# The first stage of a hybrid encoder layer: who loads the vectors, how the early weight columns arrive, and in what order x is turned

## The chip, the cores and the metric

One core of a Trainium2 chip runs the whole program. The metric is device time in microseconds (us); the kernel before took 2727.44 us (median of three runs, 2724.23 to 2729.16). TensorE (PE) multiplies, with weight loads shown apart (PEld); VectorE (DVE), ScalarE (ACT) and GpSimd (POOL) work beside it; SyncE (SP) issues most DMAs. Everything is float32, and each large product is made of float32r pieces.

## The reference

One layer for 512 prompt frames and 64 sample frames (two independent sequences, with their own condition vectors c), model width 2048:

```python
mod = silu(c) @ w_ada + b_ada                 # (2, 6*2048): sh1, sc1, g1, sh2, sc2, g2
h   = rmsnorm(x, norm1) * (1 + sc1) + sh1
proj = h @ w_in                               # columns a_q, a_k, a_v, a_r, a_lr, b_q, b_k, ...
# gated linear attention and gated DeltaNet on the columns of proj, heads normed and gated
x = x + g1 * (concat(o_a, o_b) @ w_out)
h = rmsnorm(x, norm2) * (1 + sc2) + sh2
x = x + g2 * conv_ffn(h)                      # w_up, causal conv of width 3, silu, w_down
y = rmsnorm(x, final_norm)                    # plus the new recurrent and conv states
```

The change touches only the first stage: `mod` (its parts sh1 and sc1), `h`, and the first columns of `proj`.

## The kernel before, in words

**Layout.** h is held transposed: 16 tiles k of 128 model columns by 576 frames (two halves of 288). A product of one weight tile 128x128 with one h tile is six matmuls (`mm6`, L735): weight and h are each split into a rounded high part and a remainder (`wh`, `wl`; `hh`, `hl`), and wh·hh, wh·hl, wl·hh are summed, for two halves each. ACT makes the high part, DVE the remainder (`pair_split`, L1132; `shift_x`, L767).

**The first stage** is `head` (L857). It does three things that depend on one another:

- *x*: five row blocks (four of 128 prompt frames, one of 64 sample frames) are loaded in four pieces each (`x_load`, L866). ACT squares them for the row sums (`x_square`), GpSimd takes the power -1/2 of each block's mean (`x_norm`, through `rsqrt`, L188), PE turns the blocks into xT (`x_turn`, L897), and the results in PSUM are copied out by ACT and DVE in turn. `x_lengths` (L889) spreads the row factors over all partitions into `rb`, which needs all five powers.
- *modulation* (`modulation`, L960): the columns of w_ada for sc1 and sh1 pass through PE in 48 pieces ("ada pieces": `hraw<-in_w_ada` loads and `bank<-hraw,cs` matmuls). After the four pieces of one half, DVE copies the sums (`rw`, L984), PE transposes them (`bank<-consts,rw`, L2423), DVE reduces and adds b_ada (`msum`, `mod`), and for sc1 makes `s`. Then DVE makes `tmp` = xT·s·rb (`scale_x`, L762), and ACT and DVE make `hh` and `hl`.
- *early products*: six column blocks of 128 columns (EARLY, L57) and 66 narrow columns (`ps_nar`, L1262) are multiplied with h while h comes into being. The 16 h tiles go in six groups of 2, 2, 3, 4, 3, 2 (GROUPS, L56), called group 0 to 5 here. For each group three pairs of column blocks are loaded (`pair_load`, L1122), split and multiplied, and the ada pieces of the next group are spread between these products (`product`, L1066).

**What sets the order.** Each engine runs its own queue in order. The order on each comes from the order of the code, moved by a scheduler that places an instruction by its estimate of when its inputs are there; a few are tied by hand (`issue_after`). SP's queue is in order, too, and a load waits there until its buffer is free: 9 buffers `hraw` (w_ada pieces and narrow weights, in a ring), 3 buffers `raw` for pairs. Seven groups of small vectors (c, b_ada, norms, conv weights, states) are loaded by `v_load` as rows (L811) and turned into columns by `v_turn` (PE L819, DVE L820).

**GpSimd before** has little to do here: memsets, then the reload of its code that precedes the powers (the second ISA row below), then the five powers.

Of the kernel before, what the change touches and what calls it, by code (L numbers as in the profile page):

```python
# [16 lines left out]
P = 128  # L17
# [39 lines left out]
EARLY = (("q", OFF_BQ, 0), ("aq", OFF_AQ, 0), ("ak", OFF_AK, 0), ("aq", OFF_AQ, 1), ("ak", OFF_AK, 1), ("aq", OFF_AQ, 2))  # L57
# [57 lines left out]
class Kern:  # L115
# [673 lines left out]
    def load_vectors(self):  # L789
# [17 lines left out]
        def load(g):  # L807
            rt = self.hslot(places[g], [P, P])
            at = 0
            for name, ap, n in groups[g]:  # L810
                nc.sync.dma_start(rt[at:at + n], ap)  # L811
                self.vmap[name] = cols[:, g, at:at + n]
                at += n
            rows_of[g] = rt, at
# [13 lines left out]
    def raw(self):  # L828
        return self.wp.tile([P, 1024], F32, tag="raw", bufs=3, name=self.name("raw"))

# [26 lines left out]
    def head(self, pool):  # L857
# [5 lines left out]
        xt, ms, squared = {}, {}, []  # L863
# [9 lines left out]
        def x_square(b):  # L873
            n = P if b < 4 else TS
            ms[b] = pool.tile([P, 8], F32, tag="ms4", bufs=5, name=self.name("ms4"))
            for q in range(4):
                A.activation(junk[:n], xt[b][q][:n], AF.Square, scale=float(D) ** -0.5, accum_out=ms[b][:n, q:q + 1])
                squared.append(last())
# [18 lines left out]
        def x_turn(b):  # L897
            n = P if b < 4 else TS
            per = 4 if b < 4 else 8
            for k0 in range(0, KD, per):  # L900
                ps = self.pgt()[:, 0]
                for k in range(k0, k0 + per):
                    with self.tc.issue_after(summed[0]) if summed else nullcontext():
                        T.transpose(ps[:, (k - k0) * n:(k - k0 + 1) * n], xt[b][k // 4][:n, k % 4 * P:(k % 4 + 1) * P],
                                    self.c["ident"][:n, :n])
                even = k0 // per % 2 == 0
                put = (lambda o, x: A.activation(o, x, AF.Copy)) if even else V.tensor_copy
                ahead = 4 * b + (8 if k0 // per < 2 else 10)
                with self.tc.issue_after(squared[min(len(squared), ahead) - 1]):
                    if b < 4:  # L910
                        put(xT[:, k0:k0 + per, b // 2, (b % 2) * P:(b % 2 + 1) * P], ps.rearrange("p (k t) -> p k t", k=per))
                    else:
                        for h in range(2):
                            put(xT[:, k0:k0 + per, h, HP:HT], ps.rearrange("p (k h t) -> p k h t", k=per, h=2)[:, :, h])
# [10 lines left out]
        v_turn(0)  # L925

# [23 lines left out]
        def ada_fill():  # L950
            while len(got) < len(todo):
                if len(got) % 8 == 0:
                    g = len(got) // 8
                    w_ahead(3 if g == 1 else 3 * g - 2)
# [5 lines left out]
        def modulation(g):  # L960
# [3 lines left out]
            for n0 in range(8 * g, 8 * g + 8, together):  # L964
# [13 lines left out]
                summed[:] = [last]  # L978
# [39 lines left out]
        first, summed, self.split_of = modulation(0), [], None  # L1018
        ada_ahead(2)
        x_load(3)  # L1020
        x_load(4)
        ada_ahead(4)
        v_load(1)
        ada_ahead(7)
        w_ahead(1)
        nar = self.narrow_load(*GROUPS[0])
        x_square(0)
        x_norm(0)
        x_square(1)
        for b in range(5):  # L1030
            if b < 4:
                x_norm(b + 1)
# [3 lines left out]
            x_diag(b)  # L1036
            if b > 0:
                next(first)
            if b == 3:
                v_turn(1)  # L1040
        x_lengths()
        for k in range(2):
            scale(k)
# [11 lines left out]
        w_ahead(2)  # L1055
        ps_nar = self.ps_nar = self.pm.tile([P, 2, 512], F32, tag="nar", bufs=1, name="ps_nar")
        accs = [pool.tile([P, 2, HT], F32, tag=f"acc{e}", bufs=1, name=f"acc{e}") for e in range(len(EARLY))]

        for g, (m0, nm) in enumerate(GROUPS):
            ks = range(m0, m0 + nm)  # L1060
            end = g == len(GROUPS) - 1
            mods = iter(()) if end else modulation(g + 1)
            units = nm * len(EARLY)
            done = stepped = 0

            def product(e, j, k):  # L1066
                nonlocal done, stepped
# [3 lines left out]
                while stepped < 7 and (stepped - 1) * (units - nm - 2) < 6 * done:  # L1071
                    r = next(mods, None)
                    stepped += 1
                    if stepped == 4 and not end:
                        for i in range(2):
                            scale(m0 + nm + i)
                    if r is WAIT:
                        break

            for e in range(0, len(EARLY), 2):  # L1080
                w = begun.pop(0) if begun else self.pair_split(*raws[3 * g + e // 2])
                ps = [self.pgt() for _ in range(2)]
                if e == 0:
                    for k in ks:
                        if k == len(self.h):
                            make(k)
                        self.mm_narrow(k, nar[:, k - m0])
                        for j in range(2):
                            product(e, j, k)
                        if k == ks[1]:  # L1090
                            w_ahead(3 * g + 3)
# [7 lines left out]
                for j in range(2):  # L1099
                    if e == 4 and not end and j == 0:  # L1100
                        nar = self.narrow_split(pool, self.narrow_load(*GROUPS[g + 1]))
                        begun.append(self.pair_split(*raws[3 * g + 3]))
                        self.split_of = last()
                    for k in ks:
# [7 lines left out]
                        if k == ks[1] and j == 0:  # L1112
                            w_ahead(3 * g + e // 2 + 3)
# [8 lines left out]
    def pair_load(self, offs, k0, n):  # L1122

        raw, w = self.raw(), n * P
        for e, off in enumerate(offs):
            self.nc.sync.dma_start(raw[:, e * w:(e + 1) * w].rearrange("p (k n) -> p k n", k=n), self.w_in(off)(k0, k0 + n))
# [5 lines left out]
    def pair_split(self, raw, n, order=None):  # L1132
# [9 lines left out]
        return [[x[:, e * w:(e + 1) * w].rearrange("p (k n) -> p k n", k=n) for x in (hi, lo)] for e in range(2)]  # L1142
# [1380 lines left out]
```

## Time and profile before

| | |
|---|---|
| median of three runs | 2727.44 us |
| profiled execution, own time | 2728.48 us |
| its span | 2726.8 us |
| PE busy | 2676.9 us (98%) |
| DVE busy | 2292.5 us (84%) |
| ACT busy | 1295.6 us (48%) |
| POOL busy | 479.1 us (18%) |
| DMA moved | 487.84 MB, 179 GB/s in the mean |
| first 175 us: DMA moved | 53.80 MB, 307 GB/s |

The rest of the page says where in these numbers to look: PE is busy in nearly every slice of the span but the first, and DMA is 90% busy in the first two of 40 slices only. The views used below are the windows (busy time of each engine, granted TensorE clock, DMA share and GB/s for one stretch), the timeline (start, length, instruction, and in brackets the idle time of that engine before it and what ended it), the groups by line, and the DMA issues. Times within the kernel count from the span's start.

### The profile page before, as it was taken

Reading aid. Unit: us, or ns where it says so; the run is one execution under the profiler, and the core shown is the slowest. Engines: PE = TensorE matmul, PEld = TensorE weight load, DVE = VectorE, ACT = ScalarE, POOL = GpSimd, SP = SyncE. Lnnn points to the kernel's source line nnn. Section 1 sums busy time; section 2 is a strip of 40 time slices with the busy share of each in tenths; the row PEclk is TensorE's granted clock in tenths of the full one; section 3 lists DMA queues with packets and bytes.
Section 4 is the critical chain, followed back from the end, with each engine's and each line's share of the span. In section 5 each row is a group of like instructions: output and inputs, shape, how many; then the busy total and the mean of one; then the engine's idle time right before and its main releaser. Section 6 shows DMA issues by size and latency. Waiting matters only on the chain.

```text
span 2726.8 us, 52222 instructions
## 1 busy us (share of the span) xinstructions
PE 2676.9 (98%) x20208; PEld 2612.6 (96%) x20208; DVE 2292.5 (84%) x3744; ACT 1295.6 (48%) x2316; POOL 479.1 (18%) x459
## 2 busy tenths in 40 slices
PE   7999999999999999999999999999999999999998
PEld 5699999999999999999999999999999999999998
DVE  4579899988898895688999999999999976888996
ACT  4246454555554442554545454545454544333453
POOL 0001010110001000001333333333333300000241
PEclk9999999999999999999999999999999999999999
DMA  9986555665565583634555555555555596674762
GB/s 290 354 253 187 156 166 160 172 165 152 151 179 160 162 270 92 182 99 120 153 179 153 178 155 175 157 173 160 170 162 168 161 315 185 197 223 121 237 182 81
DMA packets 646203, 487.84 MB, mean 179 GB/s; under 512 B 66601, under 2 KB 568356, under 8 KB 645956
## 3 DMA queue, kind: packets, MB, share of 16 engines
q1 hardware_dynamic: 632420, 470.25, 57.5%
q10 hardware_dynamic: 13536, 14.26, 1.8%
q8 instruction: 159, 2.61, 0.4%
q14 instruction: 88, 0.72, 0.1%
HBM read 400.38 MB, written 84.04 MB: 178 GB/s over the span
## 4 chain that ended last, share of the span: by engine, by line
PE 81%; DVE 8%; DMA 5%; issue 3%; ACT 2%; SPq 1%; POOL 0%; POOLq 0%; ACTq 0%; DVEq 0%
PE g L744 17%; PE bank L1880 16%; PE bank L1881 16%; PE bank L1882 16%; PE g L746 8%; PE bank L2427 4%; DVE wl L1790 2%; PE bank L2423 1%; DVE m L2381 1%; DMA raw<-in_w_out_dram 1%; PE bank L744 1%; DVE wl L2408 1%; DMA hraw<-in_w_ada_dram 1%; DMA raw<-in_w_in_dram 1%; PE bank L973 1%
## 5 line engine op out<-in xcount | busy, mean ns | idle before, releaser
L1880 PE MATMUL bank<-slot,wh 128*128 128x290 f32 (+1 forms) x3584 | 1063.7, 297 | 2.1 <-DVE v L1903 0.6
L1881 PE MATMUL bank<-slot,wh 128*128 128x290 f32 (+1 forms) x3584 | 1063.8, 297 | 0.0
L1882 PE MATMUL bank<-slot,wl 128*128 128x290 f32 (+1 forms) x3584 | 1058.4, 295 | 1.1 <-DVE wl L1790 0.9
L1882 PEld LDWEIGHTS bank<-slot,wl 128*128 128x128 f32 x3584 | 679.8, 190 | 2.6 <-DVE wl L1790 2.2
L1880 PEld LDWEIGHTS bank<-slot,wh 128*128 128x128 f32 x3584 | 674.4, 188 | 6.7 <-issue 6.4
L1881 PEld LDWEIGHTS bank<-slot,wh 128*128 128x128 f32 x3584 | 677.8, 189 | 0.1
L744 PE MATMUL g<-hh,wh 128*128 128x288 f32 x2048 | 468.9, 309 | 1.6 <-DVE kt L2408 0.9
L1788 ACT ACTIVATE wh<-raw 128x1024 fp32r<-128x1024 f32 (+1 forms) x304 | 280.9, 924 | 347.6 <-PE bank L1881 330.2
L746 PE MATMUL g<-hh,wl 128*128 128x288 f32 x2048 | 441.7, 296 | 2.3 <-DVE wl L1141 2.3
L744 PE MATMUL g<-hl,wh 128*128 128x288 f32 x2048 | 441.5, 296 | 0.3 <-DVE hl L775 0.2
L1790 DVE TENSOR_TENSOR wl<-raw,wh 128x1024 fp32r<-128x1024 f32 (+1 forms) x304 | 374.2, 1231 | 68.7 <-ACT wh L1788 65.6
L1788 ACT ACTIVATE wh<-s 128x1024 fp32r<-128x1024 f32 (+1 forms) x228 | 211.0, 927 | 293.9 <-PE bank L1881 133.7
L744 PEld LDWEIGHTS g<-hh,wh 128*128 128x128 f32 x2048 | 324.4, 189 | 15.8 <-issue 10.4
L746 PEld LDWEIGHTS g<-hh,wl 128*128 128x128 f32 x2048 | 329.7, 188 | 4.2 <-DVE wl L1141 2.7
L744 PEld LDWEIGHTS g<-hl,wh 128*128 128x128 f32 x2048 | 329.4, 188 | 2.7 <-issue 1.9
L1790 DVE TENSOR_TENSOR wl<-s,wh 128x1024 fp32r<-128x1024 f32 (+1 forms) x228 | 251.2, 1103 | 13.6 <-ACT wh L1788 12.5
L2408 ACT ACTIVATE wh<-raw 128x1024 fp32r<-128x1024 f32 x135 | 143.1, 1062 | 182.1 <-PE g L744 148.6
L2004 POOL TENSOR_TENSOR j<-j,j 128x288 f32<-128x288 f32 (+1 forms) x120 | 187.9, 1572 | 82.2 <-ACT j L2008 80.0
L2408 DVE TENSOR_TENSOR wl<-raw,wh 128x1024 fp32r<-128x1024 f32 x135 | 166.1, 1231 | 34.7 <-ACT wh L2408 33.5
L2408 DVE SCALAR_TENSOR_TENSOR acc<-aw,ct,acc 128x512 f32<-128x512 f32 x264 | 187.9, 745 | 1.2 <-DMA aw<-in_w_ada_dram 1.2
L2408 DVE SCALAR_TENSOR_TENSOR acc<-xr,ct,acc 128x512 f32<-128x512 f32 x216 | 154.4, 750 | 0.0
L2076 DVE TENSOR_TENSOR slot<-bank,slot 128x288 f32<-128x288 f32 x184 | 83.2, 452 | 33.3 <-PE bank L1882 32.9
(317 smaller groups left out, 3272.7 us busy)
## 6 DMA issues: line engine op xcount, KB each, us to landing
raw<-in_w_up_dram SPq DMA_DIRECT2D x176, 512.0 KB
raw<-in_w_in_dram SPq DMA_DIRECT2D x100, 512.0 KB
raw<-in_w_down_dram SPq DMA_DIRECT2D x128, 320.0 KB
slot<-cd SPq DMA_DIRECT2D x140, 288.0 KB
aw<-in_w_ada_dram SPq DMA_DIRECT2D x74, 512.0 KB
cd<-j SPq DMA_DIRECT2D x120, 288.0 KB
xr<-in_w_ada_dram SPq DMA_DIRECT2D x54, 512.0 KB
hraw<-in_w_ada_dram SPq DMA_DIRECT2D x40, 512.0 KB
```

What stands on the lines that cost most here:

```text
L744: T.matmul(ps[:, h if bank is None else bank, :n], wh, x[:, h, :n], start=f, stop=False)
L746: T.matmul(ps[:, h if bank is None else bank, :n], wl, ah[:, h, :n], start=False, stop=stop)
L973: T.matmul(ps[32 * k:32 * k + 32, :w], cs[:, k0 + k], got[n][k // per][:, k % per], start=(n == together - 1 + 8 * g + 4 * (1 - mi)), stop ...
L1788: self.nc.scalar.activation(hi, src, AF.Copy)
L1790: self.nc.vector.tensor_tensor(lo, src, hi.bitcast(F32), op=ALU.subtract)
L1880: T.matmul(ps, wh[:, j], hi, start=(c < 3 and j == 0), stop=False, skip_group_check=True)
L1881: T.matmul(ps, wh[:, j], lo, start=False, stop=False, skip_group_check=True)
L1882: T.matmul(ps, wl[:, j], hi, start=False, stop=(j == n - 1), skip_group_check=True)
L2004: minus = lambda out, a, b: G.tensor_tensor(out, a, b, op=ALU.subtract)
L2076: V.tensor_tensor(dst, ps, dst, op=ALU.add)
L2408: r = f(*a, **kw)
L2427: return self.engine.matmul(out, *a, **kw)
```

## The change

1. The vectors' 14 loads (`v_load`) are issued by GpSimd instead of SP, and the first two groups (c; b_ada, norm1, norm2) at the start.
2. EARLY is reordered, so that the second and third pair are neighbouring columns; such a pair is one transfer of 256 columns (rows of 1 KB) instead of two of 128 (rows of 512 B). The first pair stays two transfers. The split tiles are sliced differently for this.
3. Pairs may also use the two buffers `xr` (`raw_early`): five buffers in place of three. Loads of pairs, narrow weights and w_ada pieces stand in a new order, and the splits of the next group's first pair and narrow weights are made ahead of the next group's `tmp`.
4. x: the constants (with the identity for turning) are loaded first. All turned prompt blocks are copied out by DVE, the sample block by ACT. A small Silu ahead of the squares loads the table that Silu needs. The hand-tied order of turns and copies is dropped.
5. `x_norm` comes after the turn of its block, `x_lengths` between the ada pieces; the narrow products come behind the products of their tile.

The diff, cut to its core:

```diff
-EARLY = (("q", OFF_BQ, 0), ("aq", OFF_AQ, 0), ("ak", OFF_AK, 0), ("aq", OFF_AQ, 1), ("ak", OFF_AK, 1), ("aq", OFF_AQ, 2))
+EARLY = (("q", OFF_BQ, 0), ("aq", OFF_AQ, 2), ("aq", OFF_AQ, 0), ("aq", OFF_AQ, 1), ("ak", OFF_AK, 0), ("ak", OFF_AK, 1))
...
-                nc.sync.dma_start(rt[at:at + n], ap)
+                nc.gpsimd.dma_start(rt[at:at + n], ap)
...
+    def raw_early(self):
+        self.n_early = getattr(self, "n_early", -1) + 1
+        return self.xr() if self.n_early % 5 in (3, 4) else self.raw()
...
-                even = k0 // per % 2 == 0
-                put = (lambda o, x: A.activation(o, x, AF.Copy)) if even else V.tensor_copy
...
+                if b < 4:
+                    V.tensor_copy(xT[:, k0:k0 + per, b // 2, (b % 2) * P:(b % 2 + 1) * P], ps.rearrange("p (k t) -> p k t", k=per))
...
-        x_load(0)
         self.load_consts(self.cp, LONG)
-        x_load(1)
         v_load, v_turn = self.load_vectors()
         v_load(0)
-        x_load(2)
+        v_load(1)
+        for b in range(3):
+            x_load(b)
+        warm = pool.tile([P, 8], F32, tag="ms4", bufs=6, name=self.name("ms4"))
+        A.activation(warm, self.mhalf, AF.Silu)
...
+                if stepped >= 4 and e >= 2 and not end and not ready:
+                    ready = True
+                    split_next()
+                    for i in range(2):
+                        scale(m0 + nm + i)
...
-        for e, off in enumerate(offs):
-            self.nc.sync.dma_start(raw[:, e * w:(e + 1) * w].rearrange("p (k n) -> p k n", k=n), self.w_in(off)(k0, k0 + n))
+        raw, rows = self.raw_early(), slice(k0 * P, (k0 + n) * P)
+        if offs[1] == offs[0] + P:
+            self.nc.sync.dma_start(r, src(offs[0], 2 * P))
+        else:
+            for e, off in enumerate(offs):
+                self.nc.sync.dma_start(r[:, :, e * P:(e + 1) * P], src(off, P))
```

**GpSimd's queue at the start.** Before, it holds the memsets of `cs` and the narrow tiles, the reload (ISA) and the five powers (`ms`).

```order
L929 MEMSET cs 128x512
L1252 MEMSET nar_563 128x132
L1252 MEMSET nar_736 128x132
L2441 ISA
L2441 TENSOR_TENSOR ms_35_301<-ms_35_301,mhalf 128x1
L2441 TENSOR_TENSOR ms_36_309<-ms_36_309,mhalf 128x1
L2441 TENSOR_TENSOR ms_37_317<-ms_37_317,mhalf 128x1
L2441 TENSOR_TENSOR ms_42_350<-ms_42_350,mhalf 128x1
L2441 TENSOR_TENSOR ms_52_398<-ms_52_398,mhalf 64x1
```

After, five loads (c, b_ada, norms) stand ahead of those memsets, and eight more loads behind them; the end of that piece of the queue reads:

```order
L811 DMA hs_752<-in_gdn_norm_dram 1x16x8
L811 DMA hs_763<-in_ffn_conv_w_dram 88x128
L811 DMA hs_780<-in_ffn_conv_w_dram 44x128
L811 DMA hs_780<-in_ffn_conv_b_dram 44x128
L811 DMA hs_795<-in_state_gdn_conv_dram 72x128
L2459 ISA
L2459 TENSOR_TENSOR ms_18_255<-ms_18_255,mhalf 128x1
L2459 TENSOR_TENSOR ms_19_260<-ms_19_260,mhalf 128x1
L2459 TENSOR_TENSOR ms_42_322<-ms_42_322,mhalf 128x1
L811 DMA hs_798<-in_state_ffn_conv_dram 88x128
L2459 TENSOR_TENSOR ms_47_354<-ms_47_354,mhalf 128x1
L2459 TENSOR_TENSOR ms_52_387<-ms_52_387,mhalf 64x1
```

So all 14 loads and the reload now stand ahead of the last power; the loads from the sixth on wait until the piece of x that held their buffer is turned and squared.

**SP's queue between the two halves of group 2's w_ada pieces.** Before, the narrow weights, nine vector loads and one pair stand between them (`hraw_733` narrow, `hs` vectors, `raw_763` a pair, `hraw_820` and after: the second half).

```order
L948 DMA hraw_700<-in_w_ada_dram 128x2x384
L1244 DMA hraw_733<-in_w_in_dram 128x2x16 x2
L811 DMA hs_750<-in_gdn_conv_w_dram 96x128
L811 DMA hs_750<-in_gla_bg_dram 4x128
L811 DMA hs_750<-in_gla_norm_dram 2x128
L811 DMA hs_750<-in_gdn_norm_dram 1x128
L811 DMA hs_761<-in_ffn_conv_w_dram 88x128
L1126 DMA raw_763<-in_w_in_dram 128x2x128 x2
L811 DMA hs_779<-in_ffn_conv_w_dram 44x128
L811 DMA hs_779<-in_ffn_conv_b_dram 44x128
L811 DMA hs_794<-in_state_gdn_conv_dram 72x128
L811 DMA hs_797<-in_state_ffn_conv_dram 88x128
```

After, one pair and the narrow weights stand there.

```order
L952 DMA hraw_698<-in_w_ada_dram 128x2x384
L952 DMA hraw_699<-in_w_ada_dram 128x2x384
L1141 DMA raw_765<-in_w_in_dram 128x2x256
L1262 DMA hraw_800<-in_w_in_dram 128x3x16 x2
L952 DMA hraw_820<-in_w_ada_dram 128x2x384
```

The nine vector loads have left this place, and the pair is one transfer.

**PE's queue where group 1 ends.** Before, behind group 2's last ada pieces (`hraw`) PE still has the third pair of group 1 to multiply (`hh_767` and `hl_768` are group 1's), and the transpose of the modulation (`rw`) stands among those products.

```order
L973 MATMUL bank_876<-hraw_837,cs 32x384 x2
L973 MATMUL bank_876<-hraw_836,cs 32x384 x2
L744 MATMUL g_980<-hh_767,wh_976 128x288 x2
L744 MATMUL g_980<-hl_768,wh_976 128x288 x2
L744 MATMUL g_981<-hh_767,wh_976 128x288
L2423 MATMUL bank_956<-consts_227,rw_935 128x128 x3
```

After, group 1's products end ahead of the last ada pieces, and the transpose (`rw`), two vector turns (L819) and group 2's first product (`hh_1008`) follow at once.

```order
L746 MATMUL g_992<-hh_783,wl_939 128x288 x2
L977 MATMUL bank_875<-hraw_841,cs 32x384 x2
L977 MATMUL bank_875<-hraw_840,cs 32x384 x2
L977 MATMUL bank_875<-hraw_837,cs 32x384 x2
L977 MATMUL bank_875<-hraw_836,cs 32x384 x2
L2441 MATMUL bank_971<-consts_219,rw_932 128x128 x3
L819 MATMUL bank_978<-consts_219,hs_780 128x88
L819 MATMUL bank_987<-consts_219,hs_795 128x72
L744 MATMUL g_1036<-hh_1008,wh_942 128x288 x2
```

Of group 1's products, 24 matmuls stood behind the last ada pieces before, and none does now; for group 2 it was 36, and is none now. At the end of group 0 ten product matmuls still stand behind the last ada pieces, five ahead of the transposes of `rw` and five behind them.

More of the change, by code (lines that the diff above doesn't have):

```diff
@@ L1099, in head @@
                 for j in range(2):
[L1100 to L1103, printed above, removed]
                     for k in ks:
```

82 lines of the change are left out of this document (43 added, 39 removed).

## Prediction

> **What bounds the kernel now.** The page's busy line comes first.
>
> ```profile
> PE 2676.9 (98%) x20208; PEld 2612.6 (96%) x20208; DVE 2292.5 (84%) x3744; ACT 1295.6 (48%) x2316; POOL 479.1 (18%) x459
> ```
>
> PE works in all but 49.9 us of the 2726.8 us span, so nothing that the change does on another engine counts unless PE stands still for it. The change stays in the first stage. The windows there (busy time of PE, PEld, DVE, ACT, POOL with counts; granted clock; DMA share; GB/s) say where PE is idle:
>
> ```profile
> 40.00:50.00 10.00, 10.00 (x89) 7.06 (x89) 3.21 (x10) 1.96 (x3) 0.27 (x1) 0.88 1.09 382
> 50.00:60.00 10.00, 9.54 (x80) 7.13 (x80) 3.36 (x10) 4.43 (x9) 0.00 (x0) 1.00 0.73 240
> 60.00:70.00 10.00, 7.93 (x65) 6.29 (x69) 5.92 (x14) 0.63 (x1) 0.32 (x1) 1.00 0.79 253
> 70.00:80.00 10.00, 7.91 (x66) 5.31 (x66) 5.68 (x14) 3.29 (x6) 0.00 (x0) 1.00 1.08 386
> 80.00:90.00 10.00, 10.00 (x70) 5.85 (x69) 4.76 (x10) 2.09 (x4) 0.00 (x0) 1.00 1.05 346
> 90.00:100.00 10.00, 8.81 (x66) 6.75 (x65) 5.51 (x12) 0.00 (x0) 0.26 (x1) 1.00 1.05 375
> 100.00:110.00 10.00, 7.83 (x57) 5.86 (x58) 5.45 (x10) 3.73 (x6) 0.00 (x0) 1.00 1.06 355
> 110.00:120.00 10.00, 10.00 (x86) 7.66 (x85) 6.22 (x13) 3.08 (x6) 0.00 (x0) 1.00 0.87 287
> ```
>
> From 40 us to 110 us PE is idle for 0.46 + 2.07 + 2.09 + 1.19 + 2.17 = 8.0 us, and from 110 us on it is full. DMA is full too (share 1.05 and more) but for 50 to 70 us, where it ran at 0.73 and 0.79: there 0.48 of 10 us went unused, 4.8 us of transfers, just ahead of PE's longest stops. So these 8.0 us, and the time up to the first product, are all that the change can act on. The timeline of PE names the stops; in brackets stand the idle time and what ended it.
>
> ```profile
> 55.93 0.54 PE L744 MATMUL g<-hh,wh 128*128 128x288 f32 x2 [0.26 <-ACT hh L772]
> 56.68 0.53 PE L744 MATMUL g<-hl,wh 128*128 128x288 f32 x2 [0.21 <-DVE hl L775]
> ...
> 67.29 0.53 PE L746 MATMUL g<-hh,wl 128*128 128x288 f32 x2 [2.07 <-DVE wl L1141]
> ...
> 72.01 0.29 PE L819 MATMUL bank<-consts,hs 88*128 88x88 f32 x1 [0.36 <-DVE cols L820]
> 73.80 1.50 PE L973 MATMUL bank<-hraw,cs 128*32 128x384 f32 x16 [1.50 <-DMA hraw<-in_w_ada_dram]
> ...
> 89.27 1.04 PE L973 MATMUL bank<-hraw,cs 128*32 128x512 f32 x2
> ...
> 100.20 1.92 PE L973 MATMUL bank<-hraw,cs 128*32 128x512 f32 x16 [1.39 <-DMA hraw<-in_w_ada_dram]
> ...
> 106.07 0.66 PE L2423 MATMUL bank<-consts,rw 128*128 128x128 f32 x4 [1.60 <-DVE rw L984]
> ```
>
> 55.93 is group 1's first product. 67.29 waits for a weight remainder that DVE makes late, behind `tmp`; 73.80 and 100.20 wait for w_ada pieces that landed late; 106.07 waits for DVE's copy of the sums. Three mechanisms, then: a late split, late transfers, and the modulation chain at a group's end.
>
> **The change part by part.**
>
> *The vectors leave SP.* SP's timeline in the place where nine of them stood:
>
> ```profile
> 54.86 0.46 SPq L811 DMA_DIRECT2D hs<-in_gdn_conv_w_dram  x1
> ...
> 61.57 0.36 SPq L811 DMA_DIRECT2D hs<-in_state_ffn_conv_dram  x1
> 62.03 4.16 SPq L948 DMA_DIRECT2D hraw<-in_w_ada_dram  x8
> ```
>
> SP spent 54.86 to 61.93 on nine vector loads, their waits and one pair, and only then began group 2's second half of w_ada, the one that PE waits for at 73.80. At about 0.4 us each the nine are 3.4 us. This is longer than the 1.50 us wait, and the DMA has room for it. But an earlier issue isn't an earlier landing in full, since DMA is at 1.08 when these pieces move; I leave 0.5 us of the wait (bounds 0 and 1.5). The vectors of the later groups now move in the prelude: by the shapes in SP's queue 439 rows of 128 floats, 0.225 MB, 0.6 us at 382 GB/s. The prelude's ends are +0.7 us and, with the order of its loads changed, −1.0; I take +0.4, nearer to the bytes, since the same x and w_ada bytes must land before the first product.
>
> [...]
>
> *The split ahead of `tmp`.* The remainder `wl` that PE waits for at 67.29 is now made ahead of `tmp`, with its raw data in one of five buffers: the 2.07 us go. What is late next is `rw`, below.
>
> *Group ends.* PE's queue now has the last ada pieces directly ahead of the next group's first product (groups 1 and 2), where products covered the chain ada sums, `rw`, transposes, `mod`, `tmp`, `hh`. That chain stands uncovered once in before, in front of the first product:
>
> ```profile
> 33.04 2.23 PE L973 MATMUL bank<-hraw,cs 128*32 128x256 f32 x32
> 36.03 0.44 PE L2423 MATMUL bank<-consts,rw 128*128 128x128 f32 x2 [0.76 <-DVE rw L984]
> 37.97 0.44 PE L1262 MATMUL ps_nar<-hh,nar 128*66 128x288 f32 x2 [1.50 <-ACT hh L772]
> ```
>
> It leaves PE idle for 0.76 + 1.50 = 2.26 us. So each group end is priced as 2.26 us less what still stands in it. The length of a product matmul comes from these starts, 0.26 us for two:
>
> ```profile
> 43.30 0.43 PE L744 MATMUL g<-hh,wh 128*128 128x288 f32 x2
> 43.56 0.43 PE L744 MATMUL g<-hl,wh 128*128 128x288 f32 x2
> ```
>
> - Group 0 to 1: ten products of 0.13 us cover 1.3: 0.9 us, where 0.26 + 0.21 stood: +0.4.
> - Group 1 to 2: two vector turns of 0.29 us (row 72.01) cover 0.6: 1.7 us new. Gone are the 2.07 and 2.09 of the windows 60 to 80; left is the 0.5 from above: −4.2 + 1.7 + 0.5 = −2.0.
> - Group 2 to 3: nothing covers: 2.3 us new; gone are the 3.4 of the windows 90 to 110 (the 1.39 and 1.60 among them): −1.1.
> - Row 89.27: two of these matmuls take 1.04 us, where 16 take 1.92 (row 100.20), so 0.24 for two; I read the 0.8 us as a wait for a late piece that the record doesn't show as idle: −0.8.
>
> The bounds of the new ends are 0 (the chain starts earlier, since PE is given the ada pieces as soon as they land) and 2.26 each.
>
> *x turned by DVE.* Eight more copies of prompt blocks:
>
> ```profile
> L911 DVE COPY xT<-g 128x512 f32<-128x512 f32 x8 | 5.5, 691 | 8.2 <-PE g L904 8.2
> ```
>
> They are 8 × 0.69 = 5.5 us of DVE in the stretch before the first product, spread over some 20 us in which the loads of x pace PE's turns; ACT is freed of as many. I price it at 0; without that cover it costs at most the last block's two copies, 1.4 us. Joined pairs (24 transfers where 36 were) move the same bytes: 0. The rest (Silu's table, the place of the narrow products, order of EARLY) moves nothing that PE waits for: 0.
>
> *GpSimd's queue.* Its timeline holds memsets and the five powers:
>
> ```profile
> 1.26 0.36 POOL L1252 MEMSET nar<- 128x132 f32 x2
> 9.24 0.56 POOL L2441 TENSOR_TENSOR ms<-ms,mhalf 128x1 f32<-128x1 f32 x1 [7.62 <-DVE ms L2408]
> ...
> 28.03 0.54 POOL L2441 TENSOR_TENSOR ms<-ms,mhalf 64x1 f32<-64x1 f32 x1 [3.18 <-DVE ms L2408]
> ```
>
> Now 14 loads and the reload stand ahead of the last power, which ended at 28.57 us. Behind a late power wait the diagonal, the lengths on PE, the ada pieces queued behind those, `tmp` and the first product. Neither the price of a load on GpSimd (d) nor that of the reload (r) has a row of its own. For d the nearest are SP's 0.36 us (row 61.57) and the longest small GpSimd instruction:
>
> ```profile
> L2441 POOL TENSOR_TENSOR kt<-kt,mhalf 128x4 f32<-128x4 f32 x2 | 3.7, 1833 | 8.6 <-DVE kt L2408 6.6 <-PE bank L2423 2.0
> ```
>
> so 0.36 to 1.83; I take the middle, 1.1. The reload lay somewhere in the 7.62 us ahead of the first power: 0 to 7.62, middle 3.8. Memsets end at 1.6, powers take 5 × 0.55 = 2.8: 4.4. Together 14 × 1.1 + 3.8 + 4.4 = 23.6 us, 5.0 us before the last power was ready. Cost 0.
>
> [...]
>
> *Sum:* +0.4 (prelude) +0.4 −2.0 −1.1 −0.8 = −3.1 us on the profiled execution's 2728.48: 2725.4. The median of before lies 1.04 lower, so 2724.3.
>
> **The rivals.**
>
> *The DMA stays full and the chain is ahead (better).* With five pair buffers and SP free, w_ada lands so early that its pieces run well ahead of the group's end and the new holes (0.9 + 1.7 + 2.3 = 4.9 us) stay at some 0.2; and the loads' new order brings the first product forward by 1.0 rather than putting it back by 0.4. For it: 4.8 us of unused DMA ahead of the stops. Against it: the w_ada pieces now stand late in PE's queue itself. Gain 3.1 + 4.7 + 1.4 = 9.2: 2718.
>
> *Only issuing moves.* The waits at 73.80 and 100.20 stay, because the transfers and not SP end them, and the new holes (4.9) outweigh the 2.07 that the split saves and the 1.60 and 0.47 that they replace: +0.8, 2728.2. For it: DMA share over 1.05 in four of the seven windows.
>
> *GpSimd's queue is late (slower).* The place is the last powers, the decision point 14 d + r + 4.4 = 28.6 us: d = 1.45 with r at 3.8, d = 1.18 with r at 7.62. With both upper ends the queue ends at 25.6 + 7.6 + 4.4 = 37.7, 9.1 us late. Nothing on PE fills that, as the ada pieces stand behind the lengths. 9.1 − 3.1 = +6.0: 2733.4. For it: loads now stand between x and PE on an engine that had nothing to do. Against it: the middle prices leave 5.0 us.
>
> **How the numbers follow.** The forecast, a gain between 1 and 5.4 us, gets 0.37; the better rival 0.35, since several terms are bounded by zero on that side; the issuing rival 0.10; the late queue 0.18. About 0.2% (5.45 us) is what a measurement of this kernel can tell from no change. Below 2722.0 lies the better rival alone: faster 0.35. Within 0.2% lie forecast and issuing rival: 0.47. Slower, above 2732.9: 0.18. The range runs from 2717.0, a little under the better rival's time, to 2733.0, just short of the late queue's: of the 0.35 some 0.08 lies below, of the 0.18 some 0.11 above. The forecast's own range is 2722 to 2726.5.
>
> **What would show it.** In the timeline after: the last `ms` power on GpSimd before 28.6 us and the first product between 37 and 38.7 (a late queue shows as powers back to back, released by POOL's queue, and a product after 40); no wait of `wl` near 67; the DMA share of 50 to 70 us above 0.9; the wait for `hraw` in the group before 80 under 0.5; idle of about 0.9, 1.7 and 2.3 us ahead of the first products of groups 1, 2 and 3, released by `rw` and `hh`; a full PE from group 3 on, with each product as long as before. The forecast is wrong if those three holes are under 0.5 us each, if the first product moves by over 1.5 us, or if the time changes behind the first stage.

## The result and the profile after

The changed kernel takes 2743.39 us (median of six runs, 2740.28 to 2746.06), the kernel before 2727.78 us beside it: a ratio of 1.0057, 95% interval 1.0044 to 1.0070. It is slower by some 0.6%, beyond the upper end of the range (2733.0). In the profiled executions the span is 2739.3 us against 2726.8, 12.5 us more. At an early matmul of the second stage that both have, the changed kernel is 11.0 us late, 188.2 against 177.2, so nearly all of the profiled difference arises in the first stage, as that part of the prediction had it. Group by group:

| first product of | before | after | later by | this stretch added |
|---|---|---|---|---|
| group 0 | 37.97 | 40.20 | 2.23 | 2.23 |
| group 1 | 55.93 | 61.23 | 5.30 | 3.07 |
| group 2 | 79.27 | 85.00 | 5.73 | 0.43 |
| group 3 | 109.87 | 117.19 | 7.32 | 1.59 |
| second stage | 177.2 | 188.2 | 11.0 | 3.7 |

The windows of the changed kernel, columns as in the prediction. Look at PE's busy time, the first number behind the length, and at the granted clock, the last but two.

```profile
50.00:60.00 10.00, 8.14 (x76) 6.41 (x75) 4.20 (x13) 3.79 (x7) 0.00 (x0) 1.00 0.99 317
60.00:70.00 10.00, 8.77 (x62) 7.08 (x66) 4.10 (x9) 2.50 (x6) 0.32 (x1) 0.83 0.45 128
...
80.00:90.00 10.00, 6.30 (x40) 4.88 (x36) 8.09 (x19) 3.98 (x8) 0.00 (x0) 0.83 1.05 385
...
110.00:120.00 10.00, 4.67 (x30) 2.39 (x26) 8.06 (x17) 2.75 (x6) 0.00 (x0) 0.80 0.81 266
```

Two things are new: whole microseconds of idle PE at 58, 82 and 114 us, and a clock of 0.80 to 0.83 in those windows, where before had 1.00 from 50 us on. PE's timeline shows both:

```profile
40.20 1.33 PE L744 MATMUL g<-hh,wh 128*128 128x288 f32 x4 [1.46 <-ACT hh L772]
...
61.23 1.26 PE L744 MATMUL g<-hh,wh 128*128 128x288 f32 x4 [3.09 <-ACT hh L772]
...
62.77 0.68 PE L744 MATMUL g<-hl,wh 128*128 128x288 f32 x2
63.25 0.68 PE L746 MATMUL g<-hh,wl 128*128 128x288 f32 x2
...
66.82 0.43 PE L744 MATMUL g<-hl,wh 128*128 128x288 f32 x2
67.09 0.43 PE L746 MATMUL g<-hh,wl 128*128 128x288 f32 x2
...
81.10 0.55 PE L2441 MATMUL bank<-consts,rw 128*128 128x128 f32 x3 [0.71 <-DVE rw L987]
...
83.78 0.28 PE L819 MATMUL bank<-consts,hs 72*128 72x72 f32 x1 [2.05 <-DVE msum L994]
85.00 1.16 PE L744 MATMUL g<-hh,wh 128*128 128x288 f32 x4 [0.94 <-ACT hh L772]
...
112.05 0.66 PE L2441 MATMUL bank<-consts,rw 128*128 128x128 f32 x4 [0.84 <-DVE rw L987]
117.19 0.85 PE L744 MATMUL g<-hh,wh 128*128 128x288 f32 x2 [4.49 <-ACT hh L772]
...
175.28 0.51 PE L744 MATMUL g<-hh,wh 128*128 128x288 f32 x2 [1.74 <-DVE hraw L1178]
```

The holes ahead of groups 1, 2 and 3 are 3.09, 0.71 + 2.05 + 0.94 = 3.70 and 0.84 + 4.49 = 5.33 us. Behind the first, two products start 0.48 us apart (62.77, 63.25), and later 0.27 us apart (66.82, 67.09). The windows of 2 us behind this hole give the granted clock:

```profile
60.00:62.00 2.00, 0.77 (x3) 0.77 (x4) 1.21 (x5) 1.78 (x5) 0.00 (x0) 0.83 0.53 114
62.00:64.00 2.00, 2.00 (x11) 1.98 (x10) 0.78 (x2) 0.72 (x3) 0.00 (x0) 0.50 0.03 8
64.00:66.00 2.00, 2.00 (x19) 0.74 (x18) 0.00 (x0) 0.00 (x0) 0.00 (x0) 0.81 0.00 0
```

With 0.50 and 1.00 as the two values (0.50 in the window from 62 us, 1.00 in that from 66 us), 0.83 is 0.7 us of half clock and 0.81 is 0.8 us: 3.4 us at half in all, from 61.3 to 64.7. Worked out in the same way, the clock stands at half from 85.2 to 88.6 us behind the second hole and from 115.9 to 122.8 us in and behind the third. What fills the third hole is on DVE; first the changed kernel, then the kernel before at the same place:

```profile
111.30 0.69 DVE L987 COPY rw<-bank 128x512 f32<-128x512 f32 x1 [1.15 <-PE bank L977]
111.91 1.22 DVE L1159 TENSOR_TENSOR wl<-xr,wh 128x1024 fp32r<-128x1024 f32 x1
113.04 1.80 DVE L765 SCALAR_TENSOR_TENSOR tmp<-xT,s,rb 128x512 f32<-128x512 f32 x4
114.76 0.18 DVE L994 TENSOR_REDUCE msum<-bank 128x8 f32<-128x32 f32 x1
114.86 1.22 DVE L1159 TENSOR_TENSOR wl<-raw,wh 128x1024 fp32r<-128x1024 f32 x1
115.99 0.16 DVE L1185 TENSOR_TENSOR mod<-msum,cols 128x8 f32<-128x8 f32 x1
```

```profile
105.33 0.68 DVE L984 COPY rw<-bank 128x512 f32<-128x512 f32 x1
106.77 0.19 DVE L991 TENSOR_REDUCE msum<-bank 128x8 f32<-128x32 f32 x1 [0.75 <-PE bank L2423]
106.99 0.17 DVE L1167 TENSOR_TENSOR mod<-msum,cols 128x8 f32<-128x8 f32 x1
```

Between `rw` and `mod` stand 4.24 us of other work of DVE: two splits of 1.22 us and `tmp`, 1.80 us. `scale` is tied behind the last split that was asked for (`split_of`). Before, that was an old one, so `tmp` was made during the products; the change asks for the next pair's split first, and `tmp` moved behind it, into the chain that PE waits for.

GpSimd's timeline:

```profile
14.58 0.53 POOL L811 DMA_DIRECT2D hs<-in_state_gdn_conv_dram  x1 [1.03 <-DMA hs<-in_x_prompt_dram]
15.21 0.60 POOL L2459 TENSOR_TENSOR ms<-ms,mhalf 128x1 f32<-128x1 f32 x1
...
25.27 0.54 POOL L2459 TENSOR_TENSOR ms<-ms,mhalf 64x1 f32<-64x1 f32 x1 [1.36 <-DVE ms L2426]
```

The last load ahead of the reload stands first, the first power behind it second. Most of the loads take 0.50 to 0.55 us each (the first 0.73), the power behind the reload starts 0.1 us behind the load ahead of it, and the last power ends at 25.8 us, ahead of the 28.6 of before. The queue of GpSimd was not late.

### The profile page after: what moved, and what is told of

Same layout as the page of the kernel before. It is cut to its first block, busy times and chain, and to the rows that moved or that the text cites. A ratio compares the mean times of both kernels' runs of the same rounds, so it can differ in the third digit from the quotient of the medians.

```text
span 2739.3 us, 52212 instructions
## 1 busy us (share of the span) xinstructions
PE 2686.2 (98%) x20208; PEld 2620.5 (96%) x20208; DVE 2296.1 (84%) x3750; ACT 1288.0 (47%) x2308; POOL 484.4 (18%) x473
## 3 DMA queue, kind: packets, MB, share of 16 engines
q8 instruction: 159, 2.61, 0.4%
## 4 chain that ended last, share of the span: by engine, by line
PE 82%; DVE 9%; issue 3%; DMA 3%; ACT 1%; SPq 0%; POOL 0%; POOLq 0%; ACTq 0%; DVEq 0%
PE g L744 18%; PE bank L1898 16%; PE bank L1899 16%; PE bank L1900 16%; PE g L746 9%; PE bank L2445 4%; DVE wl L1808 2%; DVE m L2399 1%; PE bank L2441 1%; PE bank L977 1%; PE bank L744 1%; DVE wl L2426 1%; DVE acc L2426 1%; DMA raw<-in_w_out_dram 1%; DVE slot L2094 1%
## 5 line engine op out<-in xcount | busy, mean ns | idle before, releaser
L744 PEld LDWEIGHTS g<-hh,wh 128*128 128x128 f32 x2048 | 326.3, 190 | 25.4 <-issue 13.5
```

The costliest lines, as they stand in the source:

```text
L744: T.matmul(ps[:, h if bank is None else bank, :n], wh, x[:, h, :n], start=f, stop=False)
```

## The experiments

Theory A: the loss is the chain at the groups' ends, made long by `tmp` on DVE, uncovered on PE, and paid a second time by the clock behind each hole. Theory B: products and w_ada pieces on PE, or the loads, make the holes, and `tmp` is hidden. Each time stands with what its median is over that of the kernel before on the same chip, and with the ratio of the two; "mark" is how much later than in the profile of before the second stage begins (one execution each).

| run | us | over before | ratio (95%) | mark |
|---|---|---|---|---|
| the change | 2743.39 | +15.6 | 1.0057 (1.0044 to 1.0070) | +11.0 |
| 1 tmp at its old place | 2734.03 | +7.4 | 1.0026 (1.0015 to 1.0036) | +3.7 |
| 2 before, tmp late | 2724.64 | −2.0 | 0.9996 (0.9987 to 1.0005) | −2.5 |
| 3 vectors on SP | 2740.30 | +13.6 | 1.0053 (1.0039 to 1.0067) | +12.0 |
| 4 before, vectors on GpSimd | 2730.07 | +3.4 | 1.0014 (1.0005 to 1.0023) | +4.2 |
| 5 unread matmuls in the holes | 2737.88 | +11.3 | 1.0044 (1.0031 to 1.0056) | +6.8 |
| 6 narrow products first | 2740.91 | +14.3 | 1.0054 (1.0041 to 1.0068) | +8.6 |
| 7 prelude | 2744.20 | +17.6 | 1.0062 (1.0050 to 1.0075) | +13.5 |
| 8 products back | 2735.94 | +9.3 | 1.0036 (1.0023 to 1.0049) | +2.2 |
| 9 before, late vectors | 2727.72 | +1.0 | 1.0004 (0.9995 to 1.0013) | −2.9 |
| 10 the same, unread matmuls | 2726.06 | −0.7 | 0.9996 (0.9988 to 1.0005) | −2.7 |
| 11 1, 6 and some of 5 together | 2732.74 | +6.0 | 1.0020 (1.0011 to 1.0029) | −0.6 |
| 12 2 and 10 together | 2727.11 | +0.8 | 1.0002 (0.9993 to 1.0011) | −3.4 |

**1. tmp at its old place (on the changed kernel).**

```diff
                     stepped += 1
+                    if stepped == 4 and not end:
+                        for i in range(2):
+                            scale(m0 + nm + i)
...
                     split_next()
-                    for i in range(2):
-                        scale(m0 + nm + i)
```

> The changed kernel with the next group's first two tmp made again at their old place (ahead of the last sums), the splits left at their new place. Theory A (tmp stands on DVE behind a split that waits for its pair, so the chain to the first product of each group is longer, and PE's clock falls in the hole): the idle ahead of the first products of groups 1, 2, 3 falls from 3.1, 3.7 and 5.3 us to about 1.2, 2.0 and 3.0 us, and the whole comes 5 to 9 us nearer to the kernel before, 2734 to 2738 us. Theory B (the product order on PE and late w_ada pieces make the holes, tmp is hidden): no more than 2 us, 2741 to 2744.

8.2 us less over the kernel before, 7.3 at the mark. The holes are 1.73, 0.15 + 0.71 + 0.49 + 0.94 = 2.29 and 0.84 + 1.77 = 2.61 us; DVE at the third group's end reads:

```profile
107.71 0.69 DVE L987 COPY rw<-bank 128x512 f32<-128x512 f32 x1 [1.15 <-PE bank L977]
108.32 1.22 DVE L1160 TENSOR_TENSOR wl<-xr,wh 128x1024 fp32r<-128x1024 f32 x1
109.45 0.18 DVE L994 TENSOR_REDUCE msum<-bank 128x8 f32<-128x32 f32 x1
109.67 0.17 DVE L1186 TENSOR_TENSOR mod<-msum,cols 128x8 f32<-128x8 f32 x1
```

`tmp` has left the chain, and at this place the second split with it. Theory A holds; B, which allowed 2 us, falls. The holes are still longer than the 0.9, 1.7 and 2.3 us of the forecast, and behind the last two the clock still stands at half for 3.4 us each (from 81.5 and from 112.2 us).

**2. The counterpart (on the kernel before): `scale` for the next group behind the next pair's split.**

```diff
-                    if stepped == 4 and not end:
-                        for i in range(2):
-                            scale(m0 + nm + i)
...
                         self.split_of = last()
+                        for q in range(2):
+                            scale(m0 + nm + q)
```

> The kernel before with the next group's first two tmp tied behind the split of the next group's first pair, as in the changed kernel; nothing else changed. Theory A: tmp's 1.8 us enter the chain rw, msum, mod, hh at the ends of groups 0 to 4, less what PE still has of products there: 3 to 8 us slower, 2731 to 2736 us. Theory B: within 2 us of the kernel before.

No loss. Theory A as written, tmp's place alone, is wrong here: in this order PE still has products behind the last w_ada pieces, and they cover a late `tmp` (the holes ahead of groups 1 and 2 grow only to 0.79 + 0.39 and 1.24 + 0.26 us). It takes both edits together, the late `tmp` and the products moved ahead. The mark is 2.5 us earlier, and the trace shows a gain in it: the split for which PE waited 2.07 us in the kernel before now stands ahead of `tmp` on DVE, and the wait is 0.26 us.

```profile
64.46 0.53 PE L746 MATMUL g<-hh,wl 128*128 128x288 f32 x2 [0.26 <-DVE wl L1140]
...
80.00:82.00 2.00, 2.00 (x13) 0.60 (x16) 1.41 (x4) 0.95 (x2) 0.00 (x0) 0.51 1.07 412
```

The second line, a window, shows the price: behind the hole of 1.24 + 0.26 us the clock fell here too, for 3.4 us.

**3 and 4. Who issues the vectors**, on the changed kernel back to SP, on the kernel before to GpSimd; one word each:

```diff
-                nc.gpsimd.dma_start(rt[at:at + n], ap)
+                nc.sync.dma_start(rt[at:at + n], ap)
```

> The changed kernel with the vectors' 14 loads issued by SyncE at the same places of the code. If the loads on GpSimd, whose transfers land some 6 us after their issue, put the first product back by 2.2 us, that goes: first product near 38, 2741 us. If another part of the prelude does it (order of loads, turns), the first product stays at 40 or later, and SyncE's freed time is lost again: 2743 to 2746 us.

> The kernel before with the vectors' 14 loads issued by GpSimd at the same places of the code, nothing else changed. If SyncE's nine loads in the stretch from 55 to 62 us were what held back the w_ada pieces that PE waits for at 73.8, that wait goes: 1 to 4 us faster, 2724 to 2727 us. If the buffers hold them back, within 0.5 us of the kernel before. If the loads on GpSimd hurt (late vectors for the first sums), slower by 1 to 3 us.

In 3 the first product stays at 40.11, so GpSimd does not put it back; its time and the change's are not told apart. In 4 the first product came at 45.68. GpSimd's timeline of 4 shows the rival of the prediction that never came true in the change, by another mechanism than the one priced:

```profile
26.84 0.53 POOL L811 DMA_DIRECT2D hs<-in_state_ffn_conv_dram  x1 [4.24 <-ACT xT L907]
27.39 0.58 POOL L2441 TENSOR_TENSOR ms<-ms,mhalf 128x1 f32<-128x1 f32 x1
```

The load waits 4.24 us for its buffer, which holds x until ACT has copied it, and the fourth power waits behind it. Not the price of a load made the queue late, but what the load waits for. Of the 7.7 us that this cost in the profiled execution, 3.5 were back by the mark.

**5. Unread matmuls in the holes** (on the changed kernel, behind the transposes of `rw`).

```diff
+                    if mi == 0 and 0 < g < 4:
+                        idle, x = self.bank(), self.h[m0 - 1][0]
+                        for _ in range((20, 20, 30)[g - 1]):
+                            with self.after(nc.cur_bb.bb.instructions[-1]):
+                                T.matmul(idle[:, :HT], x[:, 0, :P], x[:, 0, :HT], start=True, stop=True)
```

> The changed kernel with matmuls that nobody reads on PE behind the last transposes of rw ahead of groups 1, 2 and 3 (20, 20 and 30 of 288 columns, 0.12 us each at full clock, less than the hole that stood there); nothing else changed, the output is the reference's. If the holes cost twice, by their length and by a clock that stands at half for some 4 us behind them, the matmuls behind the holes run at full length again (0.26 us for two products, not 0.48) and the time falls by 1.5 + 1.6 + 2.3 us: 2737 to 2740 us. If only the length of the holes counts, nothing changes or the dummies cost 1 us: 2742 to 2746.

4.3 us less over the kernel before (4.2 at the mark), with work added and nothing else (twenty of the unread matmuls took 2.88 us, 0.14 each, where 0.12 was expected). By the times alone this is not settled, since the two intervals overlap (1.0031 to 1.0056 here, 1.0044 to 1.0070 for the change); the traces carry it. PE's timeline around the first of the three holes:

```profile
56.67 2.88 PE L997 MATMUL bank<-hh 128*128 128x288 f32 x20
...
60.58 0.53 PE L744 MATMUL g<-hh,wh 128*128 128x288 f32 x2 [0.37 <-ACT hh L772]
...
61.70 0.42 PE L746 MATMUL g<-hh,wl 128*128 128x288 f32 x2
61.96 0.43 PE L1285 MATMUL ps_nar<-hl,nar 128*66 128x288 f32 x2
```

The products behind it start 0.26 us apart at once, where the change had 0.48, and the granted clock is 1.00 in the windows behind all three holes. In the four kernels that leave these three holes empty and as long (the change, 3, 6 and 7) the clock fell in or just behind each of the twelve; in 5 and 11, which fill them, behind none of the six. So, as an estimate from the 0.50 of the windows, a hole of the change cost its length and then half of the next 3.4 us, or of the next 5.6 us behind the third one, where the half clock lasted longer.

**6. Narrow products first** (on the changed kernel).

```diff
+                        self.mm_narrow(k, mine[:, k - m0])
                         for j in range(2):
                             product(e, j, k)
-                        self.mm_narrow(k, mine[:, k - m0])
```

> The changed kernel with the narrow products ahead of the products of their tile again, as in the kernel before. If the 1.7 us stop at the end of the stage (near 173 us, released by the last group's sums on DVE) comes from narrow products that end last and the copy of them that stands on DVE ahead of those sums, it is gone: 1 to 2.5 us faster than the changed kernel, 2741 to 2742.5. If the order of EARLY makes it, the stop stays and the time with it, 2743 to 2745.

The stop at 175 us is gone and the mark is 2.4 us earlier; the time is 1.3 us nearer to the kernel before, which the intervals do not tell apart. DVE in the changed kernel, in that stop:

```profile
173.06 0.76 DVE L1178 SCALAR_TENSOR_TENSOR hraw<-g,acc 128x256 f32<-128x256 f32 x2 [2.40 <-PE g L746]
173.73 0.74 DVE L1112 COPY xr<-ps_nar 64x576 f32<-64x576 f32 x1
174.40 0.74 DVE L1182 SCALAR_TENSOR_TENSOR xr<-g,acc 128x576 f32<-128x576 f32 x1
175.06 0.21 DVE L1178 SCALAR_TENSOR_TENSOR hraw<-g,acc 128x64 f32<-128x64 f32 x1
```

The copy of the narrow sums stands between the pieces of the sum whose PSUM tile the next product needs.

**7. Prelude** (on the changed kernel).

```diff
-        ada_ahead(6)
-        w_ahead(1)
-        ada_ahead(8)
+        ada_ahead(8)
+        w_ahead(1)
...
+            self.powered = last()
...
-                nc.gpsimd.dma_start(rt[at:at + n], ap)
+                with self.after(self.powered if g > 1 else None):
+                    nc.gpsimd.dma_start(rt[at:at + n], ap)
```

> The changed kernel with two changes of what moves ahead of the first product: the eight w_ada pieces of group 0 ahead of the first pair's load, and vector groups 2 to 6 tied behind the last power on GpSimd. If the first product stands 2.2 us later because 0.25 MB of vectors and 0.25 MB of weights move ahead of the last w_ada piece (at 0.32 MB per us), it comes back to 38.5 to 39 us, and the time falls by 1 to 2 us to 2741 to 2742.5. If the turns, powers or clock set it, it stays at 40.

Between the two: PE starts the last piece at 35.46 (36.43 in the change), the first product at 39.38 (40.20), and the time does not fall. The half megabyte explains 1.0 us of the late landing at most. What makes the rest was not found. The mark is 2.5 us later than in the change although the first product is earlier: the hole ahead of group 1 is 3.88 us long (3.09 in the change), and in this execution the clock stood at half for 6.8 us at the holes ahead of groups 1 and 2, twice as long as in the change.

**8. Products back** (on run 1).

```diff
-                    w_ahead(3 if g == 1 else 3 * g - 1)
+                    w_ahead(3 if g == 1 else 3 * g - 2)
...
-                if stepped >= 4 and e >= 2 and not end and not ready:
-                    ready = True
-                    split_next()
...
-                            w_ahead(3 * g + 4)
+                            w_ahead(3 * g + 3)
...
-                            w_ahead(3 * g + e // 2 + 4)
+                            w_ahead(3 * g + e // 2 + 3)
...
+                    if e == 4 and not end and j == 0:
+                        split_next()
```

> The kernel of the first experiment (tmp at its old place) with pairs loaded one step less far ahead and the next pair's split at its old place, by which PE's queue gets products back behind the last w_ada pieces (20 at the end of group 1 in place of none, 42 at the end of group 2). Theory: the chain of the modulation was covered by those products, and a short hole keeps the clock up. Holes ahead of groups 2 and 3 under 0.6 us (1.9 and 2.6 in the first experiment), no half clock behind them: 3 to 6 us faster than the first experiment, 2728 to 2731 us. If the loads one step less ahead make PE wait for pairs, 2733 or more.

A miss: no faster than run 1, though the mark is 1.5 us earlier. The holes at the groups' ends shrink to 0.83 us ahead of group 1 and 0.58 us at the end of group 2, but PE waits for w_ada again, and the clock falls behind that wait as well:

```profile
74.53 2.79 PE L977 MATMUL bank<-hraw,cs 128*32 128x384 f32 x16 [1.77 <-DMA hraw<-in_w_ada_dram]
...
101.43 3.53 PE L977 MATMUL bank<-hraw,cs 128*32 128x512 f32 x16 [1.81 <-DMA hraw<-in_w_ada_dram]
```

The same two groups took 1.50 and 1.92 us in the kernel before. With products ahead of the pieces PE stood for the chain, with products behind them it stood for the pieces.

**9 and 10. The kernel before with late vectors** (groups 2 to 6 on GpSimd, tied behind the last power as in 7, groups 0 and 1 on SP), and with unread matmuls ahead of the first product:

```diff
+                if n0 == 7:
+                    idle = self.bank()
+                    idling(idle, 4, last)
                 with self.after(multiplied[-1] if g > 0 else None), ...
                     pc = self.transpose4(...)
+                if n0 == 7:
+                    idling(idle, 8)
```

> The kernel before with vector groups 2 to 6 issued by GpSimd behind the last power (groups 0 and 1 stay on SyncE); nothing else changed. In the fourth experiment the loads on GpSimd put the first product back by 7.7 us, since the fourth power stood behind a load that waited for its buffer, and the whole won 3.4 us back of it in the groups behind. If both readings are right, the first product stays at 38 and the 3 us are kept: 2723 to 2725 us. If SyncE's relief was worth nothing and the 3.4 us came from what the delay let land, 2726 to 2728.

> The ninth kernel with 4 + 8 small matmuls that nobody reads on PE in the hole between the last w_ada piece of group 0 and the first product (in the trace of before 0.76 + 1.50 us idle, then a clock of 0.5 to 43 us: 18 products at 0.24 us in place of 0.13 and one group of pieces at 1.51 in place of 1.07). If the hole alone brings the clock down, they keep it up, and the time falls by another 1.5 to 2.4 us, to 2721 to 2723.5. If the clock was decided earlier, by the gaps between 30 and 36 us, it stays low and the time stays within 0.5 us of the ninth kernel or rises by the dummies' own 0.5 us.

In 9 the 2.07 us wait for `wl` is gone, the wait for w_ada ahead of 70.78 is 0.28 us (1.50 before), and the second stage begins 2.9 us earlier. Not all of this is SP's: on DVE the split now stands ahead of `tmp` (64.04 and 65.39; in the kernel before 66.55 and 64.83), the same gain that run 2 has. From group 1's first product to the w_ada group at 70.78 it takes 14.3 us here, 17.9 in the kernel before (55.93 to 73.80) and 16.5 in run 2 (54.74 to 71.21), which has the split alone: by these, one execution each, some 2 us are SP's. Yet the time is that of the kernel before; in its profile the span is 1.0 us shorter. Behind the first stage, places that no edit touched differ by a few us from profile to profile, 3.3 us of them in 9 within one stretch near 1210 us. For 10, the window behind the hole, of 9 and then of 10:

```profile
40.00:42.00 2.00, 2.00 (x12) 1.99 (x11) 1.52 (x4) 0.60 (x2) 0.00 (x0) 0.62 1.09 386
```

```profile
40.00:42.00 2.00, 2.00 (x24) 1.25 (x23) 1.23 (x3) 0.32 (x1) 0.00 (x0) 1.00 1.07 379
```

Clock 1.00 for 0.62, twice the matmuls in the same 2 us. That the filling did it is likely but not shown: in run 2 the same hole, empty (1.05 + 1.50 us), also left the clock at 1.00. Group 0 took 16.33 us (38.56 to 54.89) in place of 17.68 (38.81 to 56.49). The 1.35 us were given back by the mark: the waits for w_ada came to 0.81 + 1.00 us where 9 had 0.28 + 0.77 + 0.26, and from the transposes at 101.80 to the next w_ada group it took 6.2 us (4.7 in 9), for the clock was down again behind those stops (0.96 in the window from 80 to 120 us).

**11. Run 1, run 6 and shorter fillings (8, 8, 11) together.**

> The changed kernel with three mendings together: tmp at its old place, narrow products first, and unread matmuls in what is left of the three holes (8, 8 and 11). One by one they brought 9.4, 2.5 and 5.5 us; the last overlaps with the first, which shortens the holes (half of the 5.5 stays). If the account of the loss is complete but for the first product's 2 us, 2728 to 2730 us. If it stays above 2732, something else costs that these three do not touch.

The second stage begins 0.6 us earlier than in the kernel before, although the first product is still 1.5 us late: the three together win back all of the 11.0 us at the mark. The time stays 6.0 us above, as the expectation had it for a cost that these three do not touch. In its profile, 5.4 us are lost between the mark and the end, in stages that the change does not name but whose order the scheduler laid anew; one of them is a stop ahead of a matmul near 985 us, 2.83 us where before had 1.46. The rest was not traced.

**12. Runs 2 and 10 together.**

> The kernel before with the three edits that did not lose by themselves: vector groups 2 to 6 on GpSimd behind the last power, unread matmuls in the hole ahead of the first product, and tmp tied behind the next split (which there leaves products and w_ada pieces as they are). In their traces the stage ended 2.9, 2.7 (both first edits) and 2.4 us earlier than before. If these add, the stage ends 4 to 5 us earlier and the time is 2722 to 2724 us, a version that beats both; if the w_ada pieces at 70 and 97 us are held by the DMA, which is full there in all three, the gains are the same gain taken twice: 2724 to 2727.

The gains are in part one gain: runs 2 and 9 both take away the same 2.07 us wait for `wl`. The mark is 3.4 us early, not 5, with 1.11 us of waiting for w_ada ahead of 70.35, the hole of run 2 ahead of group 2 (1.24 us) and, behind it, 3.4 us at half clock. The time cannot be told from that of the kernel before. No version beats it clear of the noise.

## Why the prediction was wrong

- **Group ends** (forecast 0.9, 1.7, 2.3 us of new idle; measured 3.09, 3.70, 5.33). This is the step that failed first. The prediction saw that the chain would stand uncovered, and took its length, 2.26 us, from the prelude, where `tmp` is made ahead of `rw` and DVE has nothing else to do between `rw` and `mod` (rows below this item). The prediction noted that the split now stands ahead of `tmp`, and did not ask what stands behind it: `tmp`, then `msum`. Run 1 removes `tmp` from the chain: 8.2 us; run 2 shows that it costs only where PE has no products left.

DVE in the kernel before, in the prelude:

```profile
33.83 1.81 DVE L765 SCALAR_TENSOR_TENSOR tmp<-xT,s,rb 128x512 f32<-128x512 f32 x4 [0.67 <-ACT rb L895]
35.55 0.42 DVE L984 COPY rw<-bank 128x256 f32<-128x256 f32 x1
36.50 0.17 DVE L991 TENSOR_REDUCE msum<-bank 128x4 f32<-128x16 f32 x1 [0.53 <-PE bank L2423]
36.71 0.16 DVE L1167 TENSOR_TENSOR mod<-msum,cols 128x4 f32<-128x4 f32 x1
```

- **The clock** (no term; some 4.3 us by run 5, part of it gone with shorter holes). A hole was priced by its length alone. The trace of before showed that it can cost more: 0.88 in the window from 40 us, behind the prelude's hole. It showed too that a hole need not: behind stops of 2.07, 1.50, 1.39 and 1.60 us the windows of before have 1.00. The clock fell behind 3.09 us in the change (half from 61.3 to 64.7 us), behind 0.76 + 1.50 us of idle time, with 0.44 us of work between, in the kernel before, behind 1.24 + 0.26 us in run 2, and behind 1.77 us in run 8, with 0.55 and 0.36 us shortly ahead of it; no length that parts the two cases can be read from these.
- **Prelude** (+0.4; measured +2.2). PE starts the last w_ada piece at 36.43 and works 1.08 us on it at half clock (0.50 in the window from 36 to 38 us), where the piece at 32.55 took 0.64 us (1.00 in the window from 32 to 34 us). Of this, run 7 brings back 0.8 us with vectors and a pair moved together, which fits the bound of +0.7 for the vectors but does not test it alone; the rest of the loads' new order was not priced, and stays open. The prediction called itself wrong if the first product moved by over 1.5 us.
- **SP's relief and the late split** (−4.2 with 0.5 left). Right as a mechanism: the split's part shows in run 2, and SP's part in what run 9 has beyond it, one execution each. In the changed kernel both are there too (no wait for `wl` near 67, none for `hraw` in groups 1 and 2) and were eaten by the longer chain: the stretch of group 1 came out at +0.4, not −2.0, and that of group 2 at +1.6 where a gain was forecast. The share of DMA from 50 to 60 us rose from 0.73 to 0.99 and that from 60 to 70 fell from 0.79 to 0.45: loads came earlier, then stood still. That another issuer saves something shows in run 9's stage alone (some 2 us beyond run 2); its time, at a ratio of 1.0004, did not keep the gain.
- **The row of 1.04 us** (−0.8). Misread: the same two matmuls take 1.04 us in run 9 too (at 87.10), and neither trace shows a wait there. An eighth of the length of sixteen was not the price of two.
- **Narrow products** (priced at 0). They cost 1.74 us at the stage's end (run 6); the prediction gave the 0 no reason but that PE waits for nothing of this.
- **GpSimd's queue** (23.6 us forecast for its work, no delay). No delay, right; d is 0.53, not 1.1, and r under 0.2 us, since the first power behind the reload started 0.1 us behind the load ahead of it (15.21 us, the load from 14.58 for 0.53). The loads landed 3.8 to 6.8 us behind their issue. The rival's mechanism is real (run 4) where a load on GpSimd waits for a buffer.
- **"Slower" itself** had a chance of 0.18, all of it on that queue. The case that came, a longer chain that also brings the clock down, was none of the rivals.
- **Two small slips** change nothing: the nine loads on SP sum to 3.0 us by their rows, not 3.4, and the DMA share is over 1.05 in three of the seven windows, not four.

## What to carry to other kernels

When an edit takes the cover off a chain, write down what now stands on each engine between the chain's links, from the order, before taking its length from another place. Price a hole on PE by its length and, as a risk, by the matmuls behind it at half clock, for the 3.4 us measured here: the empty holes of 3 us and more at the groups' ends (the change, runs 3, 6 and 7) all brought the clock down, and those of 1.2 to 2.6 us (runs 1 and 2) some of the time. A cost that is covered twice may show nothing when one cover goes: run both halves alone and together, and read the mark behind the stage as well as the end.

## What was not expected of the hardware

The clock fell behind stops as short as 1.24 + 0.26 us (run 2) and stayed up behind one of 2.07 us (before), so the length of a stop alone does not decide it here. By the windows from 20 to 190 us, once down it stayed down for 3.4 us in the kernel before (from 39.1 us), and in the change for 3.4 us twice (from 61.3 and 85.2), 6.8 us twice (from 23.8 and 115.9) and 10.2 us (from 34.0). Eight to thirty matmuls that nobody reads, placed in each hole, went with a clock of 1.00 behind it (runs 5 and 11); on the changed kernel they were worth some 4.3 us. In the change a load issued by GpSimd took 0.5 us of its queue and 3.8 to 6.8 us to land. From 40 to 48 us DMA moved 350 GB/s in the changed kernel and 380 in the kernel before at the same share of about 1.09; why was not found.
